# Layer 2's S5 parameters and tables built during layer 1's feed-forward stage, reciprocal roots by a GpSimd power

## The chip, the cores and the metric

The kernel runs on one core of one Trainium2 chip. The metric is device time in microseconds (us), the median of 3 runs. The span of a profile is the time from the program's first to its last instruction; the profiled execution's own time is a little longer than its span. Engine names: PE is TensorE (PEld its weight loads), DVE is VectorE, ACT is ScalarE, POOL is GpSimd, SP is SyncE, whose queue issues most loads.

## The reference

An encoder of two layers works on 512 tokens of width 1024, in fp32. Each layer:

```
h = rms_norm(x); q, k, v, u_f, u_s, gates = split(h @ w_in)
y_a = rms_norm(diff_attention(rotary(q), rotary(k), v)) @ w_attn      # 8 heads
y_b = fourier_mix(u_f) @ w_four
y_c = glu(gelu(s5_mix(u_s)))                                          # state-space layer, 32 groups, 2 directions
x = x + (gates . (y_a, y_b, y_c)) @ w_out
h = rms_norm(x); x = x + (gelu(conv(h @ w_up_gate)) * (h @ w_up)) @ w_down
h = rms_norm(x); x = x + sigmoid(h @ w_pg) * (p @ w_ple)
```

A last rms_norm follows. `s5_mix` is a diagonal complex recurrence: its matrices depend on the layer's parameters alone (`ssm_a`, `ssm_log_dt`, `ssm_b`, `ssm_c`), not on the tokens. So everything that is made of them (here "parameters" and "tables") can be computed at any time before the recurrence.

## The kernel before

Matrix products take fp32 values as a high and a low half (`split`, L75; `unit`, L85): a weight tile of 128x1024 is loaded by SP into `wr` (two buffers), ACT copies the high halves `wh` (L94), DVE subtracts them to give `wl` (L95; six buffers of each, 512 columns wide), and `mm` (L101) issues three matmuls per 128 rows. A "unit" is 24 matmuls of 512 columns into one of three PSUM banks `w`. The scheduler of the language orders each engine's instructions ahead of time, by the order in which the program emits them and by explicit priorities (`high_priority` with a negative offset makes work wait behind later emitted work); at run time every engine and every queue goes through its own list in order.

A layer (`layer`, L750) runs as stages: the norm (`norm`, L150), the projections of u_s and u_f (`s5_load_u`, `fourier`), eight heads of attention with their projections (`v_pair`, `qk_proj`, `head`), the S5 recurrence in eight chunks of four groups (`s5_chunk`, L616) with gates beside it, the branches, the gated feed-forward stage (22 steps f of two up units each, then 8 down products k of 22 blocks), and the per-layer embedding.

In each layer the S5 work that depends on parameters alone lies inside the mixing stages. `s5_params` (L274) makes 144 small DVE instructions, most of 64 elements, and 24 POOL instructions, among the projections. `s5_tables` (L373) runs once per chunk, at low priority, beside the heads (chunks 0 and 1 at head 0, then one per head): eight products of 512 elements on POOL (L400, L401, L417, L418), two sums on DVE (L402) feeding eight matmuls against the identity and C (L410, each shows as two matmul instructions) through the single PSUM bank `m`, ACT evacuations (L411, L412), two more sums (L419), and the rotation tables by 12 POOL instructions in `cmul` (L238 to L243). Six DMAs on ACT's queue write the chunk's 1.5 MB table to DRAM, from where `s5_chunk` reads it. `s5_toeplitz` (L440) ends the job with 15 DMAs of `dtab`. Its tile pool `gen` lives until the heads are done.

`rsqrt` (L109) makes a reciprocal root from an integer seed and three Newton steps: eight DVE instructions (L115 to L124) on at most 4 elements per partition. It is called in six norms and sixteen heads through `rms`, and four times in the last stage.

Of the kernel before, what the change touches and what calls it, by code (L numbers as in the profile page):

```python
# [18 lines left out]
P = 128  # L19
# [31 lines left out]
class Kernel:  # L51
# [57 lines left out]
    def rsqrt(self, pool, v, n):  # L109

# [135 lines left out]
    def setup(self):  # L246
        nc, a = self.nc, self.a
        self.cp = self.pool("const")
        self.small = self.cp
        self.dp = self.pool("dram", space=DRAM)  # L250
        self.psum = self.pool("psum", space=PSUM)
        self.ident = self.t(self.cp, "ident", (P, P))
        make_identity(nc, self.ident)
        self.ones = self.t(self.cp, "ones", (P, 1))
        nc.vector.memset(self.ones, 1.0)
        self.cst = self.t(self.cp, "cst", (P, 3))
# [17 lines left out]
    def s5_params(self, i, keep, pool, R):  # L274
        nc, a = self.nc, self.a
        V = nc.vector
        n = 64
# [5 lines left out]
        nc.sync.dma_start(prm, a["s5p"][i])  # L283
# [18 lines left out]
        Wr = self.t(keep, "Wr", (P, 8, n))  # L302
        Wi = self.t(keep, "Wi", (P, 8, n))
        Br = self.t(keep, "BWr", (P, 8, n))
        Bi = self.t(keep, "BWi", (P, 8, n))
        V.tensor_tensor(out=Wr[:, 0], in0=r1, in1=c, op=ALU.mult)
        V.tensor_tensor(out=Wi[:, 0], in0=r1, in1=sn, op=ALU.mult)
# [6 lines left out]
        V.tensor_scalar(out=nr, in0=Wr[:, 0], scalar1=-1.0, scalar2=None, op0=ALU.add)  # L314
        V.tensor_tensor(out=t, in0=nr, in1=are, op=ALU.mult)
        V.tensor_tensor(out=u, in0=Wi[:, 0], in1=aim, op=ALU.mult)
        V.tensor_tensor(out=t, in0=t, in1=u, op=ALU.add)
        V.tensor_tensor(out=Br[:, 0], in0=t, in1=den, op=ALU.mult)
        V.tensor_tensor(out=t, in0=Wi[:, 0], in1=are, op=ALU.mult)
        V.tensor_tensor(out=u, in0=nr, in1=aim, op=ALU.mult)  # L320
        V.tensor_tensor(out=t, in0=t, in1=u, op=ALU.subtract)
        V.tensor_tensor(out=Bi[:, 0], in0=t, in1=den, op=ALU.mult)

        tmp = self.t(pool, "ptmp", (P, 7, n))
        G = nc.gpsimd
        for w in (1, 2, 4):
            self.cmul(G, Wr[:, w:2 * w], Wi[:, w:2 * w], Wr[:, 0:w], Wi[:, 0:w],
                      Wr[:, w - 1:w].to_broadcast([P, w, n]), Wi[:, w - 1:w].to_broadcast([P, w, n]), tmp[:, 0:w])
        self.cmul(G, Br[:, 1:8], Bi[:, 1:8], Wr[:, 0:7], Wi[:, 0:7],
                  Br[:, 0:1].to_broadcast([P, 7, n]), Bi[:, 0:1].to_broadcast([P, 7, n]), tmp)  # L330
# [12 lines left out]

        ph = []
        for q in range(2):
            co = self.t(keep, f"phc{q}", (P, n, 8))
            si = self.t(keep, f"phs{q}", (P, n, 8))
            V.memset(co[:, :, 0:1], 1.0)
            V.memset(si[:, :, 0:1], 0.0)
            f = [c8, s8] if q == 0 else [fc, fs]  # L350
            k = 1
            while True:
                b = [P, n, k]
                self.cmul(V, co[:, :, k:2 * k], si[:, :, k:2 * k], co[:, :, 0:k], si[:, :, 0:k],
                          f[0].unsqueeze(2).to_broadcast(b), f[1].unsqueeze(2).to_broadcast(b),
                          tmp.rearrange("p k n -> p (k n)")[:, :n * k].rearrange("p (n k) -> p n k", k=k))
                k *= 2
                nf = [self.t(pool, f"pf{q}{k}c", (P, n)), self.t(pool, f"pf{q}{k}s", (P, n))]
# [5 lines left out]
                if k == 8:  # L364
                    break
            fc, fs = f
            ph.append((co, si))
# [3 lines left out]
        return dict(Wr=Wr, Wi=Wi, Br=Br, Bi=Bi, ph=ph)  # L371

    def s5_tables(self, i, pool, prm, ch, kfb, cat, tab, prio):  # L373

        nc, a = self.nc, self.a
        G = nc.gpsimd
        g0 = ch * GC
        bc = self.t(pool, "bc", (P, 4, GC, 16))
        nc.sync.dma_start(bc, a["s5bc"][i, ch])

# [5 lines left out]
        full = [P, GC, 8, 16]  # L386

        def wsel(w, d, rev):
            v = w.rearrange("p k (d g) -> p d g k", d=2)[:, d, g0:g0 + GC]
# [6 lines left out]

        for d in range(2):
            vb = self.t(pool, "tb1", full, bufs=2)
            t2 = self.t(pool, "tb2", full, bufs=1)
            G.tensor_tensor(out=vb, in0=wsel(prm["Br"], d, d == 0), in1=bsel(0), op=ALU.mult)  # L400
            G.tensor_tensor(out=t2, in0=wsel(prm["Bi"], d, d == 0), in1=bsel(1), op=ALU.mult)  # L401
            nc.vector.tensor_tensor(out=vb, in0=vb, in1=t2, op=ALU.add)  # L402
            vbf = vb.rearrange("p g j h -> p g (j h)")
            with self.tc.high_priority(offset=self.tc.tile_snap_priority() - prio):

                vt = self.t(pool, "vbt", (P, GC, P), bufs=1)
                for g in range(0, GC, 2):
                    pv = self.ps("m")[:, :2 * W1].rearrange("p (g x) -> p g x", g=2)
                    for q in range(2):
                        nc.tensor.matmul(pv[:, q], lhsT=vbf[:, g + q], rhs=cat[:, g + q], start=True, stop=True)  # L410
# [3 lines left out]
        for d in range(2):  # L414
            ct = self.t(pool, "tb1", full, bufs=2)
            t2 = self.t(pool, "tb2", full, bufs=1)
            G.tensor_tensor(out=ct, in0=wsel(prm["Wr"], d, d == 1), in1=bsel(2), op=ALU.mult)  # L417
            G.tensor_tensor(out=t2, in0=wsel(prm["Wi"], d, d == 1), in1=bsel(3), op=ALU.mult)  # L418
# [4 lines left out]
        full = [P, GC, 8, 8]  # L423
        co = self.t(pool, "tb1", (P, 2, GC, 8, 8), bufs=2)
        si = self.t(pool, "tb1", (P, 2, GC, 8, 8), bufs=2)
        for d in range(2):
            lo = [x.rearrange("p (d g) k -> p d g k", d=2)[:, d, g0:g0 + GC].unsqueeze(2).to_broadcast(full)
                  for x in prm["ph"][0]]
            hi = [x.rearrange("p (d g) k -> p d g k", d=2)[:, d, g0:g0 + GC].unsqueeze(3).to_broadcast(full)
                  for x in prm["ph"][1]]  # L430
            t2 = self.t(pool, "tb2", (P, 512), bufs=1)[:, 0:256].rearrange("p (g a b) -> p g a b", g=GC, a=8)
            self.cmul(G, co[:, d], si[:, d], lo[0], lo[1], hi[0], hi[1], t2)
        co = co.rearrange("p d g a b -> p (d g a b)")
        si = si.rearrange("p d g a b -> p (d g a b)")
# [3 lines left out]
        nc.scalar.dma_start(tab[:, 2560:3072], si)  # L438

# [176 lines left out]
    def s5_chunk(self, pool, U, ch, prm_R, tab, dtab, ysd):  # L616
# [12 lines left out]
        rv = prm_R.rearrange("p (d g) -> p d g", d=2)[:, :, g0:g0 + GC].unsqueeze(3)  # L629
# [120 lines left out]
    def layer(self, i, x):  # L750
# [15 lines left out]
        gp = self.pool(f"gen{i}", side="right")  # L766
# [15 lines left out]
        tabs = [self.t(self.dp, f"tab{ch}", (P, 3072)) for ch in range(NCH)]  # L782
        dtab = self.t(self.dp, "dtab", (P, 8, NG, 16))
        usd = self.t(self.dp, "usd", (T, T))
        ysd = self.t(self.dp, "ysd", (P, NG * NC))
        s5R = self.t(rp, "s5R", (P, 64))
        tp = self.pool(f"tmp{i}")
# [6 lines left out]
        tp.release()  # L794
        up.release()
        ar = self.pool(f"rot{i}")
        aq = self.pool(f"qk{i}")
        ap = self.pool(f"att{i}")
        kfb = self.t(gp, "kfb", (P, 2, NG, 16))
        cat = self.t(gp, "cat", (P, GC, W1))  # L800
# [419 lines left out]
```

## Time and profile before

| what | value |
|---|---|
| median of 3 runs | 2235.51 us (2234.33 to 2235.66) |
| the profiled execution, own time | 2237.99 us |
| its span | 2236.2 us |
| busy in the span: PE, DVE, ACT, POOL | 95%, 69%, 46%, 34% |
| layer 1: heads, tail to the S5 chunks, feed-forward | 110 to 410, to 447, 719 to 1076 us |
| layer 2: projections, heads, tail, feed-forward | 1150 to 1197, to 1498, to 1546, 1820 to 2170 us |

Matmuls are pipelined and the profile models their ends, so a busy share of PE is an upper bound of what PE works; how many matmuls of which width lie in a stretch, and how far apart they start when nothing holds them, is read from counts and from the chain of waits.

### The profile page before, as it was taken

How to read it: one execution, taken by the hardware profiler on the slowest of the kernel's cores; microseconds unless marked ns; L12 is line 12 of the kernel's file. 1: busy time of each engine (PE TensorE's matmuls, PEld its weight loads, DVE VectorE, ACT ScalarE, POOL GpSimd, SP SyncE). 2: the span in 40 equal slices, each digit the busy share in tenths (PEclk: the TensorE clock that was granted, in tenths of full speed). 3: DMA queues.
4: the chain of work that ended last, by engine and by line, in shares of the span. 5: the costliest groups of instructions: out<-in, count | busy, mean ns of one | idle time of the engine just before them, and what ended most of it. 6: DMA issues, size and time to landing. Idle time of an engine off the chain costs nothing.

```text
span 2236.2 us, 29074 instructions
## 1 busy us (share of the span) xinstructions
PE 2121.7 (95%) x10432; PEld 1772.2 (79%) x10432; DVE 1534.3 (69%) x2664; ACT 1023.5 (46%) x1900; POOL 760.2 (34%) x748
## 2 busy tenths in 40 slices
PE   7888989899999999999998898898999999999998
PEld 5777778688888888888887787687888888888886
DVE  7988997566666766633689899984666667665344
ACT  4256665244434444433442766552445444444333
POOL 4497876223101322200025967841330012221000
PEclk9999999999999999999998999999999999999999
DMA  5232232665323333233432322236743323333341
GB/s 186 79 110 78 86 101 97 190 222 197 116 94 95 97 102 95 92 95 97 149 118 80 105 87 90 97 123 186 259 150 107 97 90 101 97 95 96 95 130 57
DMA packets 117232, 259.20 MB, mean 116 GB/s; under 512 B 43456, under 2 KB 49856, under 8 KB 115040
## 3 DMA queue, kind: packets, MB, share of 16 engines
q1 hardware_dynamic: 87040, 218.48, 31.3%
q10 hardware_dynamic: 30048, 38.87, 5.2%
q8 instruction: 82, 1.34, 0.3%
q14 instruction: 62, 0.51, 0.1%
HBM read 216.87 MB, written 40.37 MB: 115 GB/s over the span
## 4 chain that ended last, share of the span: by engine, by line
PE 69%; DVE 13%; POOL 6%; DMA 5%; ACT 3%; issue 2%; ACTq 0%; SPq 0%; DVEq 0%; POOLq 0%
PE w L106 55%; PE s L106 5%; DVE wl L95 2%; DMA tab<-tb 1%; PE s L639 1%; DVE mx L541 1%; DMA U<-usd 1%; PE w L1079 1%; POOL ra L501 1%; POOL tb L417 1%; DVE tb L402 1%; DVE pr L553 1%; PE w L1026 1%; PE w L1028 1%; PE w L1027 1%
## 5 line engine op out<-in xcount | busy, mean ns | idle before, releaser
L95 DVE TENSOR_TENSOR wl<-wr,wh 128x512 fp32r<-128x512 f32 x596 | 465.5, 785 | 303.5 <-ACT wh L94 295.6
L94 ACT ACTIVATE wh<-wr 128x512 fp32r<-128x512 f32 x596 | 368.5, 624 | 631.4 <-PE w L106 424.7
L106 PE MATMUL w<-hh,wh 128*128 128x512 f32 x1536 | 607.8, 396 | 20.1 <-DVE rs L499 9.0
L106 PE MATMUL w<-hl,wh 128*128 128x512 f32 x1536 | 604.8, 394 | 2.3 <-DVE hl L82 2.2
L106 PE MATMUL w<-hh,wl 128*128 128x512 f32 x1536 | 604.6, 394 | 1.6 <-DVE wl L95 1.6
L106 PEld LDWEIGHTS w<-hh,wh 128*128 128x128 f32 x1536 | 291.6, 190 | 82.5 <-DVE rs L499 10.6
L106 PEld LDWEIGHTS w<-hl,wh 128*128 128x128 f32 x1536 | 291.2, 190 | 63.5 <-DVE hl L82 5.0
L106 PEld LDWEIGHTS w<-hh,wl 128*128 128x128 f32 x1536 | 290.9, 189 | 62.0 <-DVE wl L95 2.2
L180 POOL TENSOR_TENSOR sq<-sq,sq 128x512 f32<-128x512 f32 x18 | 25.0, 1391 | 454.0 <-ACT sq L178 454.0
L191 POOL TENSOR_TENSOR ge<-ge,cv 128x512 f32<-128x512 f32 x44 | 57.8, 1315 | 305.3 <-DVE ge L190 305.3
L106 PE MATMUL w<-ah,wl 128*128 128x512 f32 x352 | 140.4, 399 | 0.0
L106 PE MATMUL w<-al,wh 128*128 128x512 f32 x352 | 138.7, 394 | 0.0
L106 PE MATMUL w<-ah,wh 128*128 128x512 f32 x352 | 138.0, 392 | 0.0
L546 ACT ACTIVATE pr<-s,mx 128x512 f32<-128x512 f32 x128 | 87.9, 689 | 54.5 <-DVE mx L541 49.2
L541 DVE TENSOR_REDUCE mx<-s 128x1 f32<-128x512 f32 x128 | 85.7, 678 | 8.9 <-PE s L540 8.9
L936 POOL TENSOR_TENSOR uu<-uu,cv 128x512 f32<-128x512 f32 x44 | 58.2, 1323 | 71.9 <-DVE cv L193 71.9
L106 PEld LDWEIGHTS w<-al,wh 128*128 128x128 f32 x352 | 66.1, 188 | 17.1
L539 PE MATMUL s<-ks,qs 128*128 128x512 f32 x128 | 56.9, 450 | 23.7 <-ACT pr L546 23.0
L106 PEld LDWEIGHTS w<-ah,wh 128*128 128x128 f32 x352 | 66.1, 188 | 15.8
L106 PEld LDWEIGHTS w<-ah,wl 128*128 128x128 f32 x352 | 66.1, 188 | 15.3
L106 PE MATMUL w<-oh,wh 128*128 128x512 f32 x128 | 52.6, 421 | 14.8 <-DVE m L841 6.5
L553 DVE SCALAR_TENSOR_TENSOR pr<-pr,c,pr 128x512 f32<-128x512 f32 x64 | 65.8, 1028 | 1.0
(417 smaller groups left out, 4227.3 us busy)
## 6 DMA issues: line engine op xcount, KB each, us to landing
wr<-in_w_in SPq DMA_DIRECT2D x112, 512.0 KB
wr<-in_w_up SPq DMA_DIRECT2D x88, 512.0 KB
tb<-tab SPq DMA_DIRECT2D x16, 1536.0 KB
tab<-tb ACTq DMA_DIRECT2D x64, 256.0 KB
wr<-in_w_down SPq DMA_DIRECT2D x32, 512.0 KB
tab<-vbt ACTq DMA_DIRECT2D x32, 256.0 KB
wr<-in_w_attn SPq DMA_DIRECT2D x16, 512.0 KB
wr<-in_w_glu SPq DMA_DIRECT2D x16, 512.0 KB
```

Source lines behind the costliest of these rows:

```text
L94: nc.scalar.activation(hi[:, :n], raw[:, c:c + n], AF.Copy)
L95: nc.vector.tensor_tensor(out=lo[:, :n], in0=raw[:, c:c + n], in1=hi[:, :n].bitcast(F32), op=ALU.subtract)
L106: nc.tensor.matmul(ps, lhsT=w[i][a], rhs=b[i], start=start and i == 0 and q == 0, stop=stop and i == n - 1 and q == 2)
L180: eng.tensor_tensor(out=sq, in0=sq, in1=acc[c], op=ALU.add)
L191: nc.gpsimd.tensor_tensor(out=sq, in0=sq, in1=y, op=ALU.mult)
L402: nc.vector.tensor_tensor(out=vb, in0=vb, in1=t2, op=ALU.add)
L417: G.tensor_tensor(out=ct, in0=wsel(prm["Wr"], d, d == 1), in1=bsel(2), op=ALU.mult)
L539: nc.tensor.matmul(s, lhsT=q[:, c, qs], rhs=kk[:, c], start=True, stop=False)
L541: V.tensor_reduce(mx[:, c:c + 1], s, op=ALU.max, axis=AX.X, negate=True)
L546: nc.scalar.activation(pt, ss[c], AF.Exp, bias=mx[:, c:c + 1], accum_out=(s1, s2)[c][:, qt:qt + 1])
L553: V.scalar_tensor_tensor(out=pr[0], in0=pr[1], scalar=c2, in1=pr[0], op0=ALU.mult, op1=ALU.add)
L936: G.tensor_tensor(out=u, in0=u, in1=c, op=ALU.mult)
```

## The change

For layer 2 (i = 1), `s5_params` and `s5_tables` run in layer 1's feed-forward stage. The parameters are emitted at the start of that stage at a priority lowered by 150; they go to DRAM in one store (`par`, 16 KB per partition) on SP's queue, and each chunk loads its part back (`prm`) on the same queue beside `bc`. `s5_steps` advances the table generator at nine points: after the up product of f = 8, 10, 13, 15, 18, 20 and after the down products k = 0, 1, 3. At each point the PE products of the chunk before are emitted first, then the sums of the next chunk; they use four PSUM banks (`m`, `o`, `t`, `s`) instead of `m` alone. `s5_toeplitz` follows the feed-forward stage. Layer 1's own tables stay beside its heads, in bank `m`. To make room, the feed-forward stage keeps two `gp` buffers instead of three, and the tiles `ah` and `al` of f = 11 to 21 take over the space of the parameters.

The parameter tables are laid out by chunk (`tab`, groups of one chunk and its eight powers together), and the rotation tables of both directions come from one `cmul` of 512 elements per operand (6 POOL instructions) instead of two of 256 (12). `rsqrt` becomes one GpSimd power with exponent -0.5; the last stage keeps the Newton steps.

```diff
     def rsqrt(self, pool, v, n):
+        y = self.t(pool, "rsq", (P, 4), bufs=4)[:, :n]
+        self.nc.gpsimd.tensor_tensor(out=y, in0=v, in1=self.mhalf[:, :n], op=ALU.pow)
+        return y
+
+    def rsqrt_steps(self, pool, v, n):
...
-    def s5_tables(self, i, pool, prm, ch, kfb, cat, tab, prio):
+    def s5_tables(self, i, ch, banks, prio=None):
...
+        if self.prm is not None:
+            prm = self.prm[:, ch]
+        else:
+            prm = self.t(pool, "pt", (P, 8, 2 * GC, 8))
+            nc.sync.dma_start(prm, self.par[:, ch])
...
+        vb = []
         for d in range(2):
...
+            G.tensor_tensor(out=v, in0=wsel(2, d, d == 0), in1=bsel(0), op=ALU.mult)
+            G.tensor_tensor(out=t2, in0=wsel(3, d, d == 0), in1=bsel(1), op=ALU.mult)
+            nc.vector.tensor_tensor(out=v, in0=v, in1=t2, op=ALU.add)
+            vb.append(v.rearrange("p g j h -> p g (j h)"))
+        yield
+        with self.tc.high_priority(offset=0 if prio is None else self.tc.tile_snap_priority() - prio):
+            for d in range(2):
...
-                    pv = self.ps("m")[:, :2 * W1].rearrange("p (g x) -> p g x", g=2)
+                    pv = self.ps(banks[d * 2 + g // 2])[:, :2 * W1].rearrange("p (g x) -> p g x", g=2)
...
+        self.cmul(G, co, si, lo[0], lo[1], hi[0], hi[1], self.t(pool, "tb2", full, bufs=1))
...
+    def s5_steps(self, i):
+
+        last = None
+        for ch in range(NCH):
+            if last is not None:
+                next(last)
+            last = self.s5_tables(i, ch, "mots")
+            next(last)
+            yield
+        next(last)
+        yield
...
-        prm = self.s5_params(i, gp, tp, s5R)
...
+        if i == 0:
+            self.s5R = self.t(self.cp, "s5R", (P, L * NC))
+            gp = self.pool(f"gen{i}", side="right")
+            tq = self.pool(f"tmp{i}")
+            self.prm = self.s5_params(i, tq, gp)
...
+            if i == 0:
+                with tc.high_priority(offset=-LOW):
+                    for ch in ([0, 1] if h == 0 else [h + 1] if h < 7 else []):
+                        for _ in self.s5_tables(i, ch, "mmmm", tc.tile_snap_priority() - LOW):
+                            pass
...
         hh, hl, rc, rb = self.norm(x, V_GFFN)
+        if i + 1 < L:
+            self.s5_begin(i + 1, self.pool(f"gen{i + 1}"))
+            steps = self.s5_steps(i + 1)
         ff = self.pool(f"ff{i}")
-        gps = [self.t(ff, f"gp{k}", (P, T + 2)) for k in range(3)]
+        gps = [self.t(ff, f"gp{k}", (P, T + 2)) for k in range(2)]
...
+        fa = self.pool(f"fa{i}")
+        fb = self.pool(f"fb{i}")
+        if i + 1 < L:
+            with tc.high_priority(offset=-LOW // 4):
+                self.prm = None
+                self.par = self.t(self.dp, "par", (P, NCH, 8, 2 * GC, 8))
+                nc.sync.dma_start(self.par, self.s5_params(i + 1, fb, fb))
+            fb.release()
+            fb = self.pool(f"fc{i}")
...
-            h = self.t(ff, "ah", dt=F32R, bufs=NF)
-            l = self.t(ff, "al", dt=F32R, bufs=NF)
+            if i + 1 < L and f in (8, 10, 13, 15, 18, 20):
+                next(steps)
+            h = self.t((fa, fb)[f // half], "ah", dt=F32R, bufs=half)
+            l = self.t((fa, fb)[f // half], "al", dt=F32R, bufs=half)
...
             V.tensor_tensor(out=x[k], in0=ps, in1=x[k], op=ALU.add)
+            if i + 1 < L and k in (0, 1, 3):
+                next(steps)
+        fb.release()
+        fa.release()
         ff.release()
+        if i + 1 < L:
+            self.s5_end(i + 1)
```

## Rows read from the trace of the kernel before

**Rows 1.** Windows: stretch, length, busy (instructions) of PE, PEld, DVE, ACT, POOL; clock, DMA, GB/s.

```profile
110.00:410.00 300.00, 271.49 (x1503) 231.13 (x1502) 259.73 (x441) 177.83 (x385) 219.93 (x215) 0.97 0.30 98
1150.00:1197.00 47.00, 36.36 (x191) 31.92 (x190) 43.70 (x128) 9.66 (x28) 24.72 (x34) 0.85 0.25 82
1197.00:1498.00 301.00, 274.44 (x1568) 236.59 (x1567) 265.18 (x472) 179.87 (x390) 215.78 (x213) 0.97 0.29 95
1498.00:1546.00 48.00, 40.40 (x198) 32.95 (x196) 21.98 (x45) 10.37 (x22) 12.66 (x17) 0.96 0.74 211
719.00:960.00 241.00, 240.98 (x1062) 198.82 (x1060) 162.06 (x245) 113.36 (x179) 57.99 (x44) 1.00 0.31 95
960.00:1076.00 116.00, 116.00 (x504) 93.68 (x503) 44.01 (x73) 38.58 (x66) 5.28 (x9) 1.00 0.36 105
```

**Rows 2.** Chain of waits in layer 1's feed-forward stage: shares, longest piece (start, us).

```profile
by line: PE w L106 99.4%; PE s L106 0.4%; PE m L132 0.2%; issue 0.0%
...
719.53 353.64 PE w L106 x1543
```

**Rows 3.** PE groups in layer 2's heads, 1197 to 1498: busy, mean ns, idle before.

```profile
L106 PE MATMUL w<-hh,wh 128*128 128x512 f32 x184 | 74.5, 405 | 3.9 <-DVE rs L499 3.9
...
L539 PE MATMUL s<-ks,qs 128*128 128x512 f32 x64 | 27.7, 438 | 9.3 <-ACT pr L546 8.8 <-ACT ks L514 0.5
...
L410 PE MATMUL m<-cat,tb 128*128 128x144 f32 x120 | 20.6, 295 | 4.9 <-DVE tb L402 4.0 <-ACT kfb L412 0.9
L1079 PE MATMUL w<-wh,hl 128*128 128x256 f32 x118 | 20.2, 284 | 0.0
...
L563 PE MATMUL o<-ath,vh 128*128 128x256 f32 x60 | 11.8, 322 | 3.3 <-ACT ath L78 3.3
```

**Rows 4.** Chain of waits in the same stretch: pieces of matmuls back to back.

```profile
1202.82 4.43 PE w L1079 x37
...
1450.66 0.89 PE m L146 x8
...
1467.59 1.42 PE o L563 x12
```

**Rows 5.** Chain of waits in layer 2's tail, 1498 to 1546: shares of the stretch.

```profile
by line: DMA U<-usd 23.4%; DMA tab<-tb 11.5%; DMA dtab<-kfb 10.0%; DMA wr<-in_w_attn 9.1%; ACTq L613 7.4%; DMA tb<-kfb 4.1%; ACTq L452 3.5%; POOL tb L243 3.1%; POOL tb L242 2.6%; POOL tb L241 2.5%; issue 2.5%; POOL tb L417 2.3%; DVE tb L419
```

**Rows 6.** DVE groups of layer 2 from 1117 to 1546: busy, mean ns, idle before.

```profile
L95 DVE TENSOR_TENSOR wl<-wr,wh 128x512 fp32r<-128x512 f32 x71 | 63.7, 905 | 25.9 <-ACT wh L94 25.8
...
L419 DVE TENSOR_TENSOR tb<-tb,tb 128x512 f32<-128x512 f32 x16 | 18.2, 1138 | 10.6 <-POOL tb L417 10.6
L402 DVE TENSOR_TENSOR tb<-tb,tb 128x512 f32<-128x512 f32 x16 | 16.1, 1007 | 0.0
...
L119 DVE SCALAR_TENSOR_TENSOR nww<-nwy 128x4 f32<-128x4 f32 x27 | 11.5, 427 | 0.6
...
L198 DVE SCALAR_TENSOR_TENSOR ex<-ex,ex 128x64 f32<-128x64 f32 (+1 forms) x21 | 5.3, 251 | 0.4
...
L340 DVE TENSOR_TENSOR p_c<-p_t,p_u 128x64 f32<-128x64 f32 x3 | 2.8, 948 | 0.1
```

**Rows 7.** POOL groups of the same stretch.

```profile
L400 POOL TENSOR_TENSOR tb<-BWr,bc 128x512 f32<-128x512 f32 x16 | 20.9, 1311 | 1.1 <-DMA tab<-tb 1.1
...
L417 POOL TENSOR_TENSOR tb<-Wr,cat 128x512 f32<-128x512 f32 x16 | 19.0, 1185 | 32.8 <-PE m L410 22.5 <-DMA tab<-tb 10.3
L243 POOL TENSOR_TENSOR tb<-tb,tb 128x256 f32<-128x256 f32 x16 | 13.8, 864 | 1.0
...
L384 POOL TENSOR_SCALAR bc<-bc 128x64 f32<-128x64 f32 x7 | 2.6, 376 | 1.9 <-DMA bc<-in_s5bc 1.8
```

**Rows 8.** DVE and POOL groups in the up part of layer 1's feed-forward, 719 to 960.

```profile
L95 DVE TENSOR_TENSOR wl<-wr,wh 128x512 fp32r<-128x512 f32 (+1 forms) x89 | 63.5, 714 | 33.3 <-ACT wh L94 29.6 <-PE w L106 2.0
...
L936 POOL TENSOR_TENSOR uu<-uu,cv 128x512 f32<-128x512 f32 x22 | 29.1, 1323 | 36.2 <-DVE cv L193 36.2
```

**Rows 9.** Waits of SP's queue in 719 to 1076: total us, times, longest.

```profile
SPq L88 <- DVE wl L95: 324.4, 66, 6.7
```

More of the change, by code (lines that the diff above doesn't have):

```diff
@@ L301, in s5_params @@
         unit(c, sn)
[L302 to L307, printed above, removed]
+        N = [P, NCH, 2 * GC]
+        v3 = lambda v: v.rearrange("p (c m) -> p c m", c=NCH)
+        tab = self.t(keep, "ptab", (P, NCH, 8, 2 * GC, 8))
+        Wr, Wi, Br, Bi = (tab[:, :, q] for q in range(4))
+        w0r, w0i, b0r, b0i = s("w0r"), s("w0i"), s("b0r"), s("b0i")
+        V.tensor_tensor(out=w0r, in0=r1, in1=c, op=ALU.mult)
+        V.tensor_tensor(out=w0i, in0=r1, in1=sn, op=ALU.mult)
         den, nr = s("den"), s("nr")
@@ L342, in s5_params @@
         unit(c8, s8)
-        ph = []
+        f = [c8, s8]
+        tv = self.t(pool, "ptmv", N + [4])
         for q in range(2):
[L346 to L358, printed above, removed]
+            co, si = tab[:, :, 4 + 2 * q], tab[:, :, 5 + 2 * q]
+            V.memset(co[..., 0:1], 1.0)
+            V.memset(si[..., 0:1], 0.0)
+            for k in (1, 2, 4):
+                bb = N + [k]
+                self.cmul(V, co[..., k:2 * k], si[..., k:2 * k], co[..., 0:k], si[..., 0:k],
+                          v3(f[0]).unsqueeze(3).to_broadcast(bb), v3(f[1]).unsqueeze(3).to_broadcast(bb),
+                          tv[..., 0:k])
+                nf = [self.t(pool, f"pf{k}c", (P, n)), self.t(pool, f"pf{k}s", (P, n))]
                 V.tensor_tensor(out=t, in0=f[0], in1=f[0], op=ALU.mult)
@@ L385, in s5_tables, with wsel @@
                         op0=ALU.mult, op1=ALU.add)
-        full = [P, GC, 8, 16]
-        def wsel(w, d, rev):
-            v = w.rearrange("p k (d g) -> p d g k", d=2)[:, d, g0:g0 + GC]
+        def wsel(q, d, rev):
+            v = prm[:, q, d * GC:(d + 1) * GC]
             if rev:
@@ L421, in s5_tables @@
                                 ct.rearrange("p g j h -> p (g j h)"))
[L423 to L434, printed above, removed]
+        full = [P, 2 * GC, 8, 8]
+        co = self.t(pool, "tb1", full, bufs=2)
+        si = self.t(pool, "tb1", full, bufs=2)
+        sel = [prm[:, q] for q in range(4, 8)]
+        lo = [v.unsqueeze(2).to_broadcast(full) for v in sel[:2]]
+        hi = [v.unsqueeze(3).to_broadcast(full) for v in sel[2:]]
+        self.cmul(G, co, si, lo[0], lo[1], hi[0], hi[1], self.t(pool, "tb2", full, bufs=1))
+        co = co.rearrange("p n a b -> p (n a b)")
+        si = si.rearrange("p n a b -> p (n a b)")
         nc.scalar.dma_start(tab[:, 2048:2560], co)
@@ L438, in s5_tables, with s5_begin, s5_end @@
         nc.scalar.dma_start(tab[:, 2560:3072], si)
+        yield
+    def s5_begin(self, i, pool):
+        kfb = self.t(pool, "kfb", (P, 2, NG, 16))
+        cat = self.t(pool, "cat", (P, GC, W1))
+        self.nc.scalar.activation(cat[:, :, :P], self.ident.unsqueeze(1).to_broadcast([P, GC, P]), AF.Copy)
+        self.tabs = [self.t(self.dp, f"tab{ch}", (P, 3072)) for ch in range(NCH)]
+        self.dtab = self.t(self.dp, "dtab", (P, 8, NG, 16))
+        self.gen = pool, kfb, cat
+    def s5_steps(self, i):
[7 more added lines that the diff above has]
+        next(last)
+        yield
+    def s5_end(self, i):
+        pool, kfb, _ = self.gen
+        self.s5_toeplitz(i, pool, kfb, self.dtab)
+        pool.release()
     def s5_toeplitz(self, i, pool, kfb, dtab):
@@ L820, in layer @@
             ol.append(r[1])
-        self.s5_toeplitz(i, gp, kfb, dtab)
-        gp.release()
+        if i == 0:
+            self.s5_end(0)
         ap.release()
@@ L918, in layer @@
         ah, al = [], []
+        half = NF // 2
+        fa = self.pool(f"fa{i}")
[7 more added lines that the diff above has]
+            fb = self.pool(f"fc{i}")
         for f in range(NF):
```

86 lines of the change are left out of this document (38 added, 48 removed).

## The prediction

> **What bounds it now.** I read the windows first. Layer 1's feed-forward stage keeps PE busy for all of its 241 and 116 us; its chain of waits is 99.4% projections, 1543 matmuls in 353.64 us, so 0.229 us each [rows 1, 2]. That is the pace of a 512-column matmul that nothing holds. Layer 2's heads look full too, 274 of 301 us, but modelled ends flatter them, so I count [rows 1, 3]: 3x184 projections and 2x64 scores of 512 columns (two half products each) at 0.229 make 155.9 us; some 354 value matmuls at 4.43/37 = 0.120, 42.4; some 177 outputs at 1.42/12 = 0.118, 20.9; the remaining 357 are small ones at 0.89/8 = 0.111, 39.7 [rows 4]. PE needs 259 of the 301 us and stands still for 42. DVE is busy for 265 of them (88%), POOL for 216 (72%) [rows 1]: PE waits on chains through two crowded engines. The reader is to see three more things: in the projections before the heads DVE is busy 43.7 of 47 us and PE lacks at least 10.6; in the tail PE lacks at least 7.6 while the chain is tables, `dtab` and the gather of U [rows 1, 5]; layer 1's heads have the same shares, 260 and 220 of 300 us, so about 44 us of idle PE [rows 1]. Only these idles can be won. PE's work is not removed by this change, it moves.
>
> **The change, part by part.** The sum is made against the profiled execution, 2237.99 us (span 2236.2); the median of 3 is 2.5 us below.
>
> *Table products.* 128 matmul instructions (120 of them in the stretch [rows 3]) at 0.111 us are 14.2 us of PE. They leave layer 2 and enter a stage in which PE never waits, so they cost there all that they save: 0.
>
> *Layer 2's heads.* DVE loses 32 table sums (16.1 + 18.2 us) and eight roots of eight instructions at about 0.43, 27.5 us [rows 6]. POOL loses about 21 us per chunk, 168 in all (eight products near 1.3, twelve of 256 elements near 0.8, three scalars [rows 7]). That matters twice: `wl` takes 905 ns in layer 2's mixing and 714 in the feed-forward stage, where POOL is busy 58 of 241 us [rows 1, 6, 8]. With two thirds of the 0.19 us back on some 66 `wl` and a little on others DVE regains 10 us. DVE then has 193 us and POOL 66, against a PE that needs 259 - 13 = 246. PE becomes the fullest engine. Idle PE goes from 42 to a value between 42 (all of it is the softmax chain, of which the scores' 8.8 us of wait for ACT is a sign [rows 3]) and 0 (as in the feed-forward stage, where DVE at 67% holds nothing). Heads keep chains that the feed-forward stage lacks, but DVE's share falls to about 74%; nearer to the lower end, I take 16: **-26**.
>
> *Projections before the heads.* About 100 of the 144 parameter instructions fall into these 47 us; without them DVE has some 20 us to do. The chains of the Fourier part stay: of 10.6 I take **-6** (ends 0, -10).
>
> *Tail.* Tables, `tab` and `dtab` leave the chain, the gather of U (23.4% of 48 us, 11 us, plus its issue) stays [rows 5]; gates run beside it: **-5** (ends 0, -7).
>
> *Roots.* The power stands nowhere in the trace. Its nearest row is a POOL scalar operation of 64 elements, 0.38 us [rows 7]; the upper bound that I allow is the 3.4 us of the DVE chain that it replaces, at which the latency would be as before. I take 0.5, on a POOL that has room in layer 2. In layer 1's heads DVE loses 27 us of 260 as well, but the tables stay there with POOL at 73%, and each power queues behind products of 1.3 us. Fewer, longer `cmul` instructions spare POOL some us per chunk. Idle 44 to 36: **-8** (ends 0, -20). In the norms the root runs beside projection matmuls: 0.
> The Trainium skill (GPSIMD Engine Reference, Engine selection) speaks against this edit: elementwise work belongs on VectorE, GpSimd being about twice slower with two inputs. By that rule alone the roots would win nothing, and the sum would be 8 us higher; the row with the 0.43 us steps says that at four elements the time is hardly paid by the element [rows 6].
>
> *The feed-forward stage, what it takes up.* Its up part runs 241 us of PE, plus 80 table matmuls of chunks 0 to 4, 9 us: 250. DVE has 162 us there [rows 1]. Added: parameters, 148 instructions between 0.25 and 0.95 us [rows 6], most by the lower value, at 0.28, 41 us (ends 35, 70); 22 sums at 1.07, 23.5; and POOL's presence. POOL's load there rises from 58 to about 58 + 18 + 5.5x21 = 191 us, as dense as in the heads, so two thirds of 176 DVE instructions with two SBUF inputs (eight per f) pay 0.19 us more: 22. DVE needs 249 of 250 us. The only rows with so dense a DVE are the heads, at 88%: 249/0.88 = 283, 33 us over PE's need. But PE here hangs on DVE only through `wl` (three units ahead) and the three `w` banks, not through a softmax, so between 0 and 33 I take **+15**.
> The Trainium skill (GPSIMD Engine Reference, Key points) says that GpSimd shares its SBUF interfaces with VectorE and contends with its two-input instructions. The `wl` rows agree, 714 against 905 ns. Without that rule and those rows DVE would need 227 us, the stall would vanish, and the sum would be 15 us lower.
>
> *Queues moved past.* SP: the 2 MB store of `par` waits for the last parameter instruction, and every later weight load queues behind it; then eight loads of `prm` and of `bc`, each waiting for a buffer that POOL frees. SP already waits 324 us in this stage for `wl` without holding PE, at most 6.7 at a time [rows 9]; two raw buffers and three split units cover about two units, 11 us. 0, and up to +10 if the store comes late. ACT: 48 table writes, 64 evacuations (about 18 us) and the 15 `dtab` writes go to an ACT that is busy 113 of 241 us: 0, up to +5 where the last ones stand before the next norm. POOL: a step of about 21 us of products queues ahead of `ge` and `uu` (1.3 us each [rows 8]); `cv`, `uu`, `ge` and now `gp` have two buffers, two f or 22 us of cover, just enough, and without it the projections' evacuations stop. The second half of `ah` waits for the parameters' space, first used at f = 11, 120 us into the stage, so hidden. DMA: 95 GB/s there, 211 in the tail without harm [rows 1]; 19 MB more over 270 us is 70 GB/s: 0.
>
> Sum: -26 - 6 - 5 - 8 + 15 = **-30**: 2208 for the profiled run, 2205 for the median.
>
> **Rivals.**
> *A, the moved work is free.* DVE keeps up beside three-deep buffers (+3) and the heads become bound by PE, idle near 3: -39 - 8 - 6 - 13 + 3 = -63, 2172. For it: the feed-forward rows have no idle today. Against: DVE's 249 of 250.
> *B, the heads hang on their own chain.* Idle in the heads falls only by 10, projections 3, tail 3, layer 1 by 5, stall +10: -11, 2224. For it: the largest named waits of PE in the heads are for the exponential, not for tables [rows 3]. Against: these sum to few us of 42.
> *C, slower: the feed-forward stage becomes bound by DVE and POOL at the heads' 88%.* +33, plus 6 where POOL's 21 us steps use up the two buffers, against -26 from heads, projections, tail and layer 1 together: +13, 2248. It decides from a stall of about 45 us with my gains, or 26 with these. For it: DVE's 99%. Against: loose coupling, and 72 us of free DVE in the down part [rows 1].
> *D, nothing moves.* Parameters come so late that the tables pile up behind the down products and the next layer waits for them as today: about 0, 2235.
> The Trainium skill (GPSIMD Engine Reference, Instruction dispatch) adds that the first call of a freshly loaded kernel costs some 6 us; if the power were one, once, in the first norm, the sum would be -24. No run here shows it.
>
> **Numbers.** Chances: forecast 0.46, A 0.21, B 0.17, C 0.11, D 0.05. The time is the forecast's. The range reaches down to A and up past B, with the upper bounds of the queues: 2172 to 2238; C and what lies beyond A stay out. This kernel's measurement tells 0.2%, 4.5 us, from no change. Faster by more: forecast, A and three quarters of B, 0.80; within: the rest of B and most of D, 0.08; slower: C and a little of D, 0.12.
>
> **What would show it.** Right: layer 2's heads some 40 us shorter (26 idle, 13 products) with DVE near 75% and POOL near 30%; `wl` near 750 ns there; layer 1's feed-forward about 29 us longer, of which 14 are table products, with `wl` near 850 ns and new waits of PE for `wl` or of evacuations; the power under 1 us. Wrong: a feed-forward stage longer by over 60 us, SP waiting over 11 us at the `par` store, or heads that keep 30 us of idle PE with DVE at 75%.

## The result, and the profile after

The changed kernel takes **2208.8 us** (median of 4 runs, 2206.19 to 2210.35) against 2235.35 us (4 runs on the same chip): a ratio of **0.9881, 95% interval 0.9864 to 0.9898**. 2205.0 had been forecast, in a range of 2172 to 2238. The profiled execution took 2210.06 us, 27.9 less than the one of before (2237.99); the sum of the prediction was 30 less. The net is right. The terms are not, so the first thing to read is where the time went, stage by stage.

The marks are the first and last instructions of a stage in the two traces (first evacuation of the up projection, last down matmul, first value projection of a head, first output projection), in us; the forecast has 13 us of table products leaving the heads and 14 entering the feed-forward stage:

```
stage                                              before    after   difference   forecast
start to layer 1's feed-forward                     718.8    701.2      -17.6         -8
layer 1's feed-forward                              347.3    409.3      +62.0        +29
its end to layer 2's heads                          115.3    110.0       -5.3         -6
layer 2's heads, to their output projection         323.8    271.2      -52.6        -39
from there to layer 2's feed-forward                314.6    301.9      -12.7         -5
layer 2's feed-forward to the end                   416.4    414.7       -1.7          0
sum (span)                                         2236.2   2208.3      -27.9        -29
```

Windows of the changed kernel, columns as in [rows 1]: layer 1's heads, feed-forward (up part, down part), projections, layer 2's heads, the tail.

```profile
131.00:392.00 261.00, 243.71 (x1380) 208.08 (x1381) 218.69 (x364) 165.48 (x365) 191.93 (x159) 0.97 0.31 101
...
701.00:980.00 279.00, 246.48 (x1069) 201.27 (x1068) 240.80 (x338) 109.36 (x208) 182.76 (x145) 0.94 0.36 116
980.00:1111.00 131.00, 126.67 (x578) 104.95 (x577) 71.62 (x87) 39.81 (x86) 66.81 (x57) 1.00 0.52 162
1189.00:1220.00 31.00, 31.00 (x165) 26.69 (x164) 20.32 (x28) 11.78 (x29) 10.53 (x14) 1.00 0.48 157
1220.00:1492.00 272.00, 266.17 (x1569) 231.98 (x1569) 196.85 (x375) 174.28 (x345) 73.56 (x55) 1.00 0.22 68
1492.00:1532.00 40.00, 36.59 (x161) 29.52 (x160) 11.57 (x19) 7.95 (x14) 1.39 (x2) 0.96 0.83 184
```

Layer 2's heads are what the prediction said: DVE at 72% (196.85 of 272) and POOL at 27%, where [rows 1] had 88% and 72%. Counted with the unit durations of [rows 2, 4], PE's 1569 matmuls need some 262 of the 272 us, so it stands idle for 10; before it was 42 of a somewhat shorter stretch. The up part is the mirror image: before, PE was busy for all of its 241 us; now it is busy for 246 of 279, with DVE at 86%, POOL at 66% and a mean granted clock of 0.94. That mean has two levels in it: for 34 us of the stage the granted clock stands at 0.5 (1.2 of 2.4 GHz), where the stage of before has 1.00 throughout. The two longest stretches at 0.5, same columns; PE is busy for 3.0 of 10.1 and 7.7 of 13.5 us in them:

```profile
881.80:891.90 10.10, 2.98 (x10) 2.42 (x10) 8.42 (x9) 3.74 (x6) 9.23 (x7) 0.50 0.35 90
956.90:970.40 13.50, 7.67 (x24) 6.49 (x25) 13.35 (x14) 5.62 (x12) 10.64 (x8) 0.50 0.26 86
```

DVE groups of the changed kernel, first in layer 2's heads, then (after the dots) in the up part, 701 to 980:

```profile
L95 DVE TENSOR_TENSOR wl<-wr,wh 128x512 fp32r<-128x512 f32 x52 | 38.6, 750 | 9.8 <-ACT wh L94 8.0 <-PE w L1140 1.8
...
L95 DVE TENSOR_TENSOR wl<-wr,wh 128x512 fp32r<-128x512 f32 x81 | 79.9, 987 | 7.3 <-ACT wh L94 7.2
L981 DVE SCALAR_TENSOR_TENSOR cv<-gp,vec,cv 128x512 f32<-128x512 f32 x22 | 20.5, 933 | 1.2 <-ACT cv L980 1.2
L982 DVE SCALAR_TENSOR_TENSOR cv<-gp,vec,cv 128x512 f32<-128x512 f32 x21 | 19.8, 941 | 0.3
L977 DVE TENSOR_TENSOR gp<-w,rstd 128x512 f32<-128x512 f32 x22 | 15.0, 684 | 0.0
L435 DVE TENSOR_TENSOR tb<-tb,tb 128x512 f32<-128x512 f32 x10 | 14.6, 1461 | 0.0
```

`wl` is at 750 ns in the heads, as forecast, and at 987 in the up part (forecast 850, [rows 8] 714). The mean hides two levels. In the trace 36 of these 81 `wl` take 0.6 to 0.7 us and 28 take over 1.1, with 17 between; before, 82 of 89 took 0.6 to 0.7. `gp`, which reads PSUM and not two tiles of SBUF, stays at 684 ns.

What PE waited for in layer 1's feed-forward stage of the changed kernel (us in total, times, longest), where [rows 2] show no wait at all:

```profile
PE m L426 <- DVE tb L416: 20.8, 3, 9.9
PE w L106 <- DVE uu L988: 5.5, 3, 3.3
PE w L106 <- DVE gp L977: 5.1, 3, 2.5
PE t L426 <- DVE tb L416: 2.9, 3, 1.1
```

So PE stops at table products whose sums aren't there, and at banks that DVE hasn't emptied. All its waits in the stage add up to 36.8 us. With 14 us for the table products, by count, some 11 of the 62 us are left; PE's matmuls at half the clock behind these waits are the likely rest, by this subtraction alone. What DVE and POOL do meanwhile shows in the timeline of 16 us from the same stage. POOL first (start, us, line; L414, L415, L433 and L434 are the tables' products, L244 to L249 the rotation, L989 and L197 the stage's own gelu multiplications):

```profile
868.04 1.74 POOL L989 TENSOR_TENSOR uu<-uu,cv 128x512 f32<-128x512 f32 x1
869.74 1.05 POOL L434 TENSOR_TENSOR tb<-pt,bc 128x512 f32<-128x512 f32 x1
872.28 1.20 POOL L244 TENSOR_TENSOR tb<-pt 128x512 f32<-128x512 f32 x1 [1.48 <-DMA tab<-tb]
873.44 1.51 POOL L245 TENSOR_TENSOR tb<-pt 128x512 f32<-128x512 f32 x1
...
878.63 1.06 POOL L248 TENSOR_TENSOR tb<-pt 128x512 f32<-128x512 f32 x1
879.77 1.59 POOL L249 TENSOR_TENSOR tb<-tb,tb 128x512 f32<-128x512 f32 x1
881.73 1.26 POOL L197 TENSOR_TENSOR ge<-ge,cv 128x512 f32<-128x512 f32 x1 [0.36 <-DVE ge L196]
```

and DVE beside it, of the same timeline:

```profile
875.54 0.75 DVE L982 SCALAR_TENSOR_TENSOR cv<-gp,vec,cv 128x512 f32<-128x512 f32 x1
878.77 1.48 DVE L95 TENSOR_TENSOR wl<-wr,wh 128x512 fp32r<-128x512 f32 x1 [2.48 <-ACT wh L94]
880.17 1.48 DVE L196 TENSOR_SCALAR ge<-ge 128x512 f32<-128x512 f32 x1
881.57 0.68 DVE L988 TENSOR_TENSOR uu<-w,rstd 128x512 f32<-128x512 f32 x1
882.17 1.37 DVE L95 TENSOR_TENSOR wl<-wr,wh 128x512 fp32r<-128x512 f32 x1
```

Between two gelu multiplications POOL has 12 us of table work, and beside it `wl` and even `ge`, with one input, take 1.4 to 1.5 us instead of 0.67 and 0.4 to 0.5. The second multiplication was not held by that work: POOL stood idle for 0.36 us until DVE's `ge` was there. Two queues moved past did no harm. The longest wait of SP for a split in this stage is 10.2 us, and the one at the store of the parameters, which had been feared, 7.2:

```profile
SPq L88 <- DVE wl L95: 259.0, 58, 10.2
...
SPq L88 <- DVE ptab L249: 7.2, 1, 7.2
```

### The profile page after: what moved, and what is told of

Read it like the earlier page. It is cut to its first block, busy times and chain, and to the rows that moved or that the text cites. A ratio compares the mean times of both kernels' runs of the same rounds, so it can differ in the third digit from the quotient of the medians.

```text
span 2208.3 us, 28788 instructions
## 1 busy us (share of the span) xinstructions
PE 2102.6 (95%) x10432; PEld 1763.5 (80%) x10432; DVE 1511.1 (68%) x2497; ACT 1014.3 (46%) x1900; POOL 780.3 (35%) x670
## 4 chain that ended last, share of the span: by engine, by line
PE 62%; DVE 15%; POOL 9%; DMA 5%; ACT 4%; issue 3%; ACTq 1%; SPq 0%; DVEq 0%; POOLq 0%
PE w L106 46%; PE s L106 5%; DVE wl L95 3%; PE w L1140 2%; PE s L679 1%; DMA tab<-tb 1%; DMA U<-usd 1%; DVE tb L416 1%; DVE tb L435 1%; PE o L603 1%; POOL ge L197 1%; POOL tb L246 1%; PE w L1087 1%; PE w L1089 1%; PE w L1088 1%
## 5 line engine op out<-in xcount | busy, mean ns | idle before, releaser
L95 DVE TENSOR_TENSOR wl<-wr,wh 128x512 fp32r<-128x512 f32 x596 | 487.3, 823 | 253.9 <-ACT wh L94 241.7
L106 PEld LDWEIGHTS w<-hh,wh 128*128 128x128 f32 x1536 | 291.2, 190 | 94.1 <-ACT wh L94 12.5
L197 POOL TENSOR_TENSOR ge<-ge,cv 128x512 f32<-128x512 f32 x44 | 62.3, 1417 | 197.4 <-DVE ge L196 197.4
L540 POOL TENSOR_TENSOR rs<-rs,sinr 128x512 f32<-128x512 f32 x32 | 48.0, 1501 | 105.1 <-DVE rs L539 92.9
L989 POOL TENSOR_TENSOR uu<-uu,cv 128x512 f32<-128x512 f32 x44 | 64.8, 1473 | 56.1 <-DVE cv L199 56.1
L112 POOL TENSOR_TENSOR rsq<-rmv,mhalf 128x4 f32<-128x4 f32 x22 | 24.8, 1128 | 149.9 <-DVE rmv L145 79.0
```

The source lines that it names most:

```text
L95: nc.vector.tensor_tensor(out=lo[:, :n], in0=raw[:, c:c + n], in1=hi[:, :n].bitcast(F32), op=ALU.subtract)
L106: nc.tensor.matmul(ps, lhsT=w[i][a], rhs=b[i], start=start and i == 0 and q == 0, stop=stop and i == n - 1 and q == 2)
L112: self.nc.gpsimd.tensor_tensor(out=y, in0=v, in1=self.mhalf[:, :n], op=ALU.pow)
L197: nc.gpsimd.tensor_tensor(out=sq, in0=sq, in1=y, op=ALU.mult)
L540: nc.gpsimd.tensor_tensor(out=rs, in0=rs, in1=sinr, op=ALU.mult)
L989: G.tensor_tensor(out=u, in0=u, in1=c, op=ALU.mult)
```

## Experiments

The question was why the feed-forward stage lost 48 us beyond the 14 of table products, and where layer 1 gained its 17.6. Unless said otherwise an edit is made to the changed kernel. The versions that leave work out were run once each, and every stage time is that of one profile. Three kernels with the same work in the stage (the changed one, the one with products at a lower priority, the one with Newton roots) show 409.3, 405.2 and 406.7 us, so a difference of less than some 5 us in the stage tells nothing.

**Leave layer 2's parameters and tables out.** Layer 2 uses layer 1's.

```diff
-            self.s5_begin(i + 1, self.pool(f"gen{i + 1}"))
-            steps = self.s5_steps(i + 1)
+            steps = iter(range(99))
...
-                nc.sync.dma_start(self.par, self.s5_params(i + 1, fb, fb))
...
-            self.s5_end(i + 1)
```

> The changed kernel without layer 2's parameters and tables (layer 2's recurrence uses layer 1's tables, so this part of the computation is left out); roots by power, two gp buffers and the split ah pools stay. In the changed kernel layer 1's feed-forward stage (first gp to last down product) takes 409 us, before it took 347. Theory W (everything added there is the table work): the stage returns to 347, the whole to 2210 - 62 = 2148. Rival G (the two gp buffers or the pools cost part of it): the stage stays over 355, the whole over 2156.

It took 2144.58 us, the stage 345.5. Two buffers of `gp` in place of three and the two pools of `ah` cost nothing by themselves (347.3 before). All 62 us are the price of the added work; whether a third `gp` buffer would lower that price was not tried.

**The parameters and their store alone.** The second hunk above stays in, the tables stay out.

> As the run without parameters and tables, but layer 2's parameters and their store to DRAM are made in the feed-forward stage; the tables are left out (layer 1's are used). Theory W with in-order waits as the main cost: the parameters cost only what PE idles in the first 110 us of the stage of the changed kernel, 7 to 9 us, so 2155 to 2158. Rival D (DVE's load as such is the cost, 41 us of parameters on a DVE with little room): 15 us or more, over 2163.

2148.14 us, the stage 352.4: the parameters cost 7 us there and 3.6 in all, less than either theory had. The tables cost the other 57, which is 14 of products, by count, and 43 of stall. The 144 small DVE instructions that the prediction priced at 41 of DVE's time were nearly free. Here `wl` of the up part is at 845 ns, between 714 and 987.

**No table products on PE.** ACT copies the sums where PE's product had stood.

```diff
+                    if prio is None:
+                        nc.scalar.activation(vt[:, g:g + 2], vb[d][:, g:g + 2], AF.Copy)
+                        nc.scalar.activation(kfb[:, d, g0 + g:g0 + g + 2], cat[:, g:g + 2, P:], AF.Copy)
+                        continue
```

> The changed kernel, in which the 128 table matmul instructions of the feed-forward stage are left out: ACT copies the sums to their destinations instead, so layer 2's S5 input matrices and kernel are not computed. DVE and POOL do all that they did. Theory P (PE, in order, waits at three table products for late sums, 24 us of named waits, and loses some 8 us more at half clock behind them): 14 us of products and about 30 of the 48 us of stall go, the stage takes 365, the whole 2166. Rival D (DVE and POOL hold the pace): only the products' 14 us and a few more go, the waits reappear before the projections, 2190 to 2196.

2228.34 us, the stage 427.6: longer by 18, which no theory had. ACT took over the waits for the sums (31.4 us at its first copy alone). So the copies were made from a constant instead.

**No table products, and nobody but POOL waits for a sum.** The two copies read `cat[:, g:g + 2, :P]` and `cat[:, g:g + 2, :16]`.

> As the run without table products, but ACT's copies read the identity and not the sums, so that neither PE nor ACT waits for a sum (layer 2's S5 input matrices and kernel are not computed); DVE makes every sum and POOL every product of the changed kernel. Theory P' (the cost is the in-order wait for late sums on whichever engine consumes them, PE in the changed kernel, ACT in the run before this one): the 14 us of products and about 30 us of stall go, stage 365, whole 2166. Rival D (the load of DVE and POOL holds the gelu chain and the evacuations whoever waits): stage over 385, whole over 2186.

2226.93 us, the stage 419.4, 10 longer than with the products. Its windows and PE's waits:

```profile
701.00:980.00 279.00, 232.83 (x949) 184.51 (x948) 256.57 (x347) 97.97 (x166) 215.40 (x167) 0.94 0.35 115
```

```profile
PE w L106 <- DVE uu L992: 37.2, 14, 5.3
PE w L106 <- DVE gp L981: 13.0, 8, 5.3
```

With nothing to hold the tables back, POOL is busy for 215 of 279 us (183 with the products) and DVE for 257 (241): more table work falls into the up part, and PE waits longer, 58 us by all its waits in place of 36.8, for its evacuations. The theory that PE's in-order wait for late sums is the cost has fallen. These waits show the lateness; they don't make it.

**Products at a lower priority.** `offset=0 if prio is None` becomes `offset=-100 if prio is None`.

> The changed kernel with the table products of the feed-forward stage emitted at a priority lowered by 100 instructions, about one f later in PE's order, so that late sums are there when PE comes to them. Theory P': PE's 24 us of waits for table sums fall under 8, the stage to about 385, the whole to about 2187. Rival D: the waits turn up before the projections, 2205 to 2215; worse if the later products hold the two tb1 buffers and with them POOL.

2207.74 us, ratio 0.9866 (0.9844 to 0.9889), the stage 405.2: as the changed kernel. PE's waits for table sums fell from 23.7 us to 17.8 only, so this edit tests little by itself.

**Leave the rotation out**, to tell POOL's load:

```diff
+        if prio is None:
+            nc.scalar.activation(co, lo[0], AF.Copy)
+            nc.scalar.activation(si, lo[1], AF.Copy)
+        else:
+            self.cmul(G, co, si, lo[0], lo[1], hi[0], hi[1], self.t(pool, "tb2", full, bufs=1))
```

> In the feed-forward stage the six rotation products of a chunk are left out of POOL (some 8.5 us a chunk, 68 us in all) and the rotation tables hold two plain copies made by ACT, so the output's second layer uses wrong rotations; sums, other products and PE's matmuls stay. Theory P, the pace is held by POOL's list, in which the gelu multiplications stand behind table products: most of the 43 us of stall goes, the stage falls from 409 to some 380 and the time to near 2180. Theory V, the pace is held by the amount of work on DVE: only the stretch of wl eases (0.95 to about 0.90 us on some 176 instructions, 9 us), the stage stays at 400 or more and the time near 2200.

2196.93 us, the stage 393.7, 15.6 less: between the two theories. **Leave the sums out** (an `if prio is not None:` ahead of both), to tell DVE's:

> In the feed-forward stage the 32 table sums are left out of DVE (about 1.05 us each, 34 us, some 24 of them beside the up part), so the second layer's tables lack their second term; POOL's products and PE's matmuls stay. Theory P (POOL's list holds the pace): at most 8 us less, the stage at 400 or more, the time 2200 to 2210. Theory V (DVE's work holds it): 25 to 34 us less, the stage near 380, the time near 2180.

2209.57 us, the stage 404.5, 4.8 less, as theory P had it and not clear of the differences between profiles. Windows of the two, without rotation and without sums:

```profile
701.00:980.00 279.00, 259.50 (x1133) 213.58 (x1132) 236.91 (x358) 119.77 (x227) 155.73 (x127) 0.95 0.39 124
```

```profile
701.00:980.00 279.00, 258.58 (x1124) 211.32 (x1123) 231.67 (x342) 111.67 (x211) 186.43 (x150) 0.96 0.39 121
```

And DVE's groups without the sums:

```profile
L95 DVE TENSOR_TENSOR wl<-wr,wh 128x512 fp32r<-128x512 f32 x84 | 86.1, 1025 | 6.5 <-ACT wh L94 6.5
L983 DVE SCALAR_TENSOR_TENSOR cv<-gp,vec,cv 128x512 f32<-128x512 f32 x22 | 28.1, 1279 | 1.5 <-ACT cv L982 1.4
L984 DVE SCALAR_TENSOR_TENSOR cv<-gp,vec,cv 128x512 f32<-128x512 f32 x22 | 25.2, 1145 | 0.5
```

26.5 us of sums left DVE in the up part (14.6 + 11.9, ten of L435 and ten of L416), and in equal windows DVE's busy time fell by 9. But the window without the sums holds 8 us of the down part. From the first to the last evacuation of `gp` the two kernels, the changed one first, have:

```profile
701.20:978.40 277.20, 244.68 (x1061) 199.78 (x1060) 239.01 (x337) 108.02 (x206) 180.96 (x143) 0.94 0.36 117
```

```profile
705.30:975.20 269.90, 249.48 (x1080) 203.81 (x1080) 222.62 (x316) 108.35 (x206) 180.51 (x146) 0.96 0.38 120
```

DVE's busy time fell by 16, so some 10 of the 26.5 us went to other instructions: `cv` went from 933 to 1279 ns and from 941 to 1145, `wl` from 987 to 1025. A busy DVE is here in part a DVE that stands beside POOL's products, and taking work from it hardly shortens the stage.

What the rotation's removal gave back can be read from the chain of one f, from the start of `gp` to the end of `al`, as a mean over f = 10 to 21 (sums of single instructions in the traces; a wait is the time from the end of the step before):

```
us per f                              before    changed   no rotation   no sums
chain, gp to al                         10.1      15.4        14.3        15.1
its five later DVE steps run             3.3       5.0         3.9         5.1
they wait                                0.4       2.0         1.7         1.1
its two POOL multiplications run         2.6       3.0         3.0         2.8
they wait                                0.2       1.4         1.4         1.6
```

POOL's in-order list holds the two multiplications back by 1.2 us more than before, 2.6 at most for one; DVE's steps take 3.4 of the 5.3 us. Without the rotation POOL's lateness stays, and DVE's steps run 1.2 us faster. In this chain, then, the gain came through DVE's speed beside POOL and not through the place in POOL's list. Of POOL's 14 products a chunk the six of the rotation carry 15.6 of the 43 us, about 2 us a chunk. If the other eight cost the same each (15.6 x 8/6 = 21), they make 36 to 37 of 43 together. That these eight do was not tried.

**Spread the steps.** Steps at `f in (9, 12, 15, 18, 21)` and `k in (1, 2, 4, 5)`, then at `f in (11, 15, 19)` and `k in (0, 1, 3, 4, 6, 7)`.

> The changed kernel with the nine table steps at f = 9, 12, 15, 18, 21 and k = 1, 2, 4, 5, so that four and not three lie in the down part and the steps of the up part are 33 us of PE apart instead of 22 to 33. Theory P': wider steps leave the sums time, but one of them is as late as today; 10 to 20 us of the 48 go, 2190 to 2200. Rival D: the same, as the load of the up part falls by a fifth, so this run does not tell them apart; it tells whether the stage can be had cheaper. If neither, 2209.

> The steps of the tables stand at f = 11, 15, 19 and k = 0, 1, 3, 4, 6, 7: six of nine in the down part, one in four f in the up part. If the up part's crowded DVE and POOL are the price and the down part still has room, the stage falls from 399 (steps in five f and four k) to near 390 and the time to about 2200. If the down part is full too, or the last tables come late for the next layer, what the up part wins is given back: 2206 to 2212.

The first: 2206.01 us, ratio 0.9858 (0.9837 to 0.9878), an interval that overlaps the changed kernel's; the stage 399.3. The second: 2210.72 us, ratio 0.9877 (0.9857 to 0.9898), the stage 383.5, 26 less than the changed kernel's, and all of it given back: from the last down matmul to layer 2's `us` it took 103.0 us in place of 79.1. The wait and the window in which that happened:

```profile
ACT rstd L172 <- DMA dtab<-kfb: 10.1, 1, 10.1
```

```profile
1086.00:1130.00 44.00, 30.06 (x113) 23.91 (x112) 25.13 (x24) 13.20 (x28) 27.16 (x21) 0.72 0.54 166
```

The last table was not made before the down part ended, ACT stood at the writes of `dtab` with the next norm behind them, and PE was busy for 30 of 44 us at a granted clock of 0.72 (in the changed kernel, for the 44 us behind its last down matmul, 42.6 at 1.00). The steps' prices come out of the three placements. From the first to the last evacuation of `gp`, against 219.4 us before and after the 7 us of parameters, the up part grew by 51 for six steps, 35 for five and 22 for three: 7 to 8.5 us a step, 1.8 of them the step's 16 products on PE. From the first to the last down matmul, against 123.4, the growth was 7.5 for three, 17.6 for four and 20.1 for six: 2.5 to 4.4 a step. That is too much for the last two, where the down matmuls begin 3 and 8 us before the last `gp`. By the whole stage, each step moved from the up to the down part took 9 to 10 us off it (409.3, 399.3, 383.5). In these two runs the evacuations of `gp` follow each other by 10.0 to 10.1 us in most f without a step behind f = 9, and by 13.8, 15.1 and 12.5 in the three f of one chunk; before it was 10.9.

**Steps as in the first, and one POOL operation a chunk to ACT.**

```diff
-        G.tensor_scalar(out=si, in0=si, scalar1=self.cst[:, 2:3], scalar2=1.0, op0=ALU.mult, op1=ALU.mult)
+        nc.scalar.activation(si, si, AF.Copy, scale=self.cst[:, 2:3])
```

> Steps as in the run with five f and four k, and the scaling of the second rotation table, one POOL operation of 512 elements a chunk, goes to ACT as a scaled copy. Theory P: eight fewer operations of about 0.8 us stand ahead of gelu multiplications, 3 to 6 us less, near 2201. Theory V: no change, near 2206; ACT has room either way.

2202.68 us (2199.43 to 2205.08), ratio **0.9845 (0.9821 to 0.9869)**, the stage 395.2: the fastest version that leaves nothing out, some 0.36% under the changed kernel by the two ratios, whose intervals still touch. The ACT edit alone (0.9858 to 0.9845) can't be told from nothing.

**The roots.** Power alone, in the kernel before; then the eight DVE steps back, in the changed one (`rsqrt_steps` in norms and heads).

> The kernel before with the roots of norms and heads by GpSimd power and nothing else changed. As forecast: 8 us in layer 1's heads and about as much in layer 2's, 2219. Rival N (the roots win nothing, GpSimd being slow on small work and crowded): 2235. Rival R (layer 1's 17.6 us of the changed kernel are all from the roots, and layer 2's heads win the same): 2200 to 2205.

> The changed kernel with the Newton roots in norms and heads. Before with the power alone won 13.7 us up to layer 1's feed-forward stage and lost some 3 us after it. Theory A: the roots are worth about the same in layer 1 here (+13 us) and nothing in layer 2's heads, where DVE has room, so about 2221. Rival B: in the feed-forward stage the power holds nothing, but layer 2's heads, rid of the tables, gain by the roots too: 2225 to 2230. Rival C: no loss, the table layout was the gain in layer 1: 2209.

Power alone: 2227.53 us, ratio 0.9964 (0.9951 to 0.9978); layer 1's feed-forward starts 13.7 us earlier, layer 2's heads take 331.1 us, 7 more than before. The time lies between the forecast's and rival N's. Without it, in the changed kernel: 2223.43, ratio 0.9943 (0.992 to 0.9966); layer 1's feed-forward starts at 721.2, 20.0 later, while the stretch from layer 1's last down matmul to layer 2's feed-forward stays (682.4 against 683.1). Of the 20, 12.2 lie in layer 1's heads (336.9 against 324.7), 2.7 ahead of them and 5.1 behind them. The 20 are those of one profiled execution that took 2226.4 us; by the two ratios the power is worth some 0.6%, 14 us. With Newton roots the new layout of the tables wins nothing in layer 1: its feed-forward starts at 721.2, before the change at 718.8. The power as the page of the changed kernel has it:

```profile
L112 POOL TENSOR_TENSOR rsq<-rmv,mhalf 128x4 f32<-128x4 f32 x22 | 24.8, 1128 | 149.9 <-DVE rmv L145 79.0
```

## Why the prediction was right, and where it was not

**The net and the direction: right**, 27.9 us against 30, by errors that cancel: 33 us too little for the feed-forward stage, 32 too little for the gains elsewhere. That the net came within some 2 us is luck.

**Layer 2's heads: the mechanism was right, the size too small.** DVE's share, POOL's share and `wl` came out as forecast and PE became the fullest engine. "I take 16" of idle was cautious: some 10 are left, and the largest wait for the softmax chain of [rows 3], 8.8 us, fell to 1.3. Rival B took that wait as the heads' own; it was DVE's and POOL's lateness. In the mark table the heads give 52.6 in place of 39.

**Projections before the heads: right** (5.3 for 6). **Tail: twice as much** (12.7 for 5). In [rows 5] the transfers of tables and `dtab` were about a quarter of the chain, with POOL's table work on top; with them gone the stretch from the first output projection to the S5 matmuls fell from 50.9 to 40.3 us, and the gather of U leads what waits are left.

**Feed-forward stage: the step that failed.** "Between 0 and 33 I take +15": it was 48, of which 43 are the tables' and 7 the parameters', with a small difference of the bare stage taken off. The loads came out nearly as forecast (DVE 241 us busy for 249, POOL 183 for 191); three things were wrong. First, the stretch. [rows 1] end the up part at 960, but the first down matmul starts at 942.7:

```profile
718.80:942.70 223.90, 223.88 (x988) 185.08 (x987) 155.37 (x233) 107.32 (x168) 56.31 (x43) 1.00 0.31 96
```

So the up part needed 224 + 9 = 233 us of PE and not 250, and 155 us of DVE in it make 242 with the prediction's additions. At the heads' 88% that is 275, 42 us over PE's need. From the first `gp` to the first down matmul it took 278, 45 over. The upper end, rightly measured, was the answer. Second, the step down from that end to 15, because PE hangs on DVE "only through `wl`" and the `w` banks: it hangs on DVE's list as well by the evacuations, and in the run without waits for sums PE stood for 50 us at `uu` and `gp`. Third, the cost beside POOL was taken as a mean of 0.19 us for two-input instructions; the mean of `wl` rose by 0.27, with the slow ones at 1.4 to 1.5 us, and `ge` with one input pays as well (0.43 us before, 0.64 here in the mean). POOL's in-order list, set at 0 with "just enough" cover, is not nothing, but in the chain of one f it is 1.2 of 5.3 us. The Trainium skill (Trainium Architecture — The Big Picture, What this means for kernel authors) says that the port pair which VectorE and GpSimd share is an exclusive lock and not a split of bandwidth. The two levels of `wl` agree with it; no run here shows the lock itself.

**Rival C** had this stage nearly right (33 and 6) and called it slower. With the forecast's gains it was to decide from a stall of about 45 us; the stall of 48 came, and the kernel was faster all the same because the gains were 76, without the 14 us of products. The sign "a stage longer by over 60" was met too, at 62: it was set as if the other terms were certain. Two signs of being right failed, `wl` near 850 ns in that stage (987) and a power under 1 us (1.13).

**Roots: right in sign, too small.** The power takes 1.13 us, twice the 0.5 taken and within its bounds. By the runs with and without it the roots bring 14 to 20 us in layer 1 and nothing in layer 2, where the tables have already left DVE; the prediction had 8, and 0 in the norms, which get some of the 7.8 outside the heads. The Trainium skill's rule that elementwise work belongs on VectorE (GPSIMD Engine Reference, Engine selection) did not decide in layer 1's heads: one POOL instruction of 1.13 us replaced eight of about 0.43 [rows 6] on the crowded engine, and won. Whether one power on DVE would win more was not tried. The first-call cost of some 6 us that the Trainium skill gives for a freshly loaded kernel (GPSIMD Engine Reference, Instruction dispatch) did not show: the first power started 0.06 us after its input and took 1.03, the longest of the 22 took 1.56.

**Queues.** SP as forecast, DMA too (116 and 162 GB/s).

**Still open:** how the 43 us divide. The chain of one f puts most on DVE's slower steps beside POOL and little on POOL's order, but no edit parts the two, and the eight table products were not left out. Why the power alone made layer 2's heads 7 us longer was not followed up.

## What to carry to other kernels

Work moved off a crowded stage is not free in a stage whose bottleneck engine never waits: look at what its helper engines' lists look like with the new work in them, and price POOL and DVE together, for part of the time taken from DVE may pass to its other instructions (here some 10 of 26.5 us). Measure a stage by its own first and last instructions before its load is weighed. Put a block of POOL work where POOL and DVE have least to do (here each step moved to the down part took 9 to 10 us off the stage), but end it before the next stage's norm, or all of it can come back. A root of a few elements is worth moving even to a slower engine when it shortens a chain on a full one.

## What the hardware showed that was not expected

- DVE's `wl` beside dense POOL products (POOL at 66%) has two main durations: 0.6 to 0.7 us (36 of 81) or over 1.1, mostly 1.4 to 1.5 (28 of 81), with 17 between; with POOL at 27%, 48 of 52 are at the lower one.
- POOL pays too: `ge` (L197) takes 1.53 us and `uu` (L989) 1.59 in this stage, in the mean, where [rows 8] have 1.32 for `uu`.
- Taking PE's table products away, with nothing left to wait for a sum, made the stage 10 us longer (419.4 for 409.3), with POOL busy for 215 us of the up part's window in place of 183: their waits seem to have held the tables' work back.
